# Feed-forward's first step: raw weights of the third and fourth pairs loaded ahead of the store of the last normalised rows

## The chip, the cores and the metric

The kernel runs on one core of one Trainium2 chip. The metric is the time of one execution in device microseconds (us). Three runs of the kernel before took 2641.86, 2644.74 and 2649.18 us; the median is 2644.74 us.

## The reference, cut to what matters

The program is a decoder trunk of two layers over 1024 tokens of width 1024, all in 32-bit floats. Each layer is a token mixer (latent attention in layer 0, a recurrent scan, RWKV-7, in layer 1) beside a memory attention, an output projection, a layer norm, a squared-ReLU feed-forward of width 4096, and a second layer norm:

```python
o = mixer(x @ w_in)                        # layer 0: attention; layer 1: RWKV scan
n = layer_norm(ALPHA * x + o @ w_out)      # these are the "normalised rows"
h = relu(n @ w_ff1) ** 2                   # first step of the feed-forward
x = layer_norm(ALPHA * n + h @ w_ff2)      # second step; reads n again
```

## The kernel before, in words

**Operands.** A 32-bit matrix is split into a high and a low part of a shorter type. ScalarE (ACT) casts the high part (L143), VectorE (DVE) subtracts it from the raw tile and writes the low part (L144). A product is then three TensorE (PE) matmuls for each tile of 128 rows: high by high, high by low, low by high. A row such as `N<-slot` of ACT L143 is the cast of the raw tile `slot` into a tile of the pool `N`; `N<-slot,N` of DVE L144 is the subtraction that belongs to it.

**The first step** is in `out_and_ff`, called once for each layer. The 1024 columns of w_ff1 by 1024 rows are multiplied with seven products of blocks instead of eight, after Strassen and Winograd, for each of 16 pairs `p` of column tiles. A pair needs products of raw blocks (A11 by B11, A12 by B21), and of sums of blocks: S3 by T3, S2 by T2, S1 by `TA`, S4 by B22, A22 by T4. The S are sums of weight blocks, formed on DVE in `blocks` (the four lines after the split of a22); the T are differences of the transposed normalised rows, formed in `second_half` and split into the tiles `TB` (T2 and T3). The rows are handled two tiles of 128 at a time, `tt` = 0, 2, 4, 6; T2 and T3 are whole only when `second_half(6, ...)` has been done.

**The early pairs.** For p = 0 to 3 the first two products (A11 by B11 and A12 by B21) run while the last rows are still being transposed: `early()` is a stream of matmuls from which `second_half` takes some between its transposes and the rest at its end. `ahead(p)` loads the raw A11 and A12 of one pair (512 KB) and splits them into `SR[0]`, two buffers that pairs 0 and 2, and 1 and 3, share. Pairs 0 and 1 land in the pool `wraw`, and their `ahead` is called before the stream. Pairs 2 and 3 land in the tile `slot` that later holds their result, and their `ahead`, the load included, is called inside the stream. In layer 0 the four slots of the pool hold the split output weights `wo[4]` and `wo[5]` until then.

**The normalised rows.** `norm` normalises two tiles of rows and stores them to the DRAM tensor `n_d`, which the second step reads again, hundreds of microseconds later. Its store is on SyncE's queue (SP), as are all loads of weights and the stores of the first step's results (`h_d`). SP takes its instructions in order: one that waits holds all behind it.

**What sets the order.** The program is not run in the order in which it is written. A scheduler with a cost model picks, for each engine, the order of the instructions over the whole program; `issue_after(x)` holds instructions back until `x` has been issued, `pin` keeps the order of matmuls as written. In layer 1 the output projection (`ps_o`, L149 to L151) is mixed by the scheduler with the matmuls of the scan, and the scan's matmuls in turn with the input projection (`ps_in`). The names `ps_y`, `ps_q` and `W` belong to the scan: `W` is its running state, updated on DVE from `ps_q` (L1202, L1209), and `ps_yo` (L1236) is a product on the scan's last result `yd` (L1222 to L1230) that ends in `o`, which is stored to `o_d` and loaded again as the last rows of the output projection's operand.

Of the kernel before, what the change touches and what calls it, by code (L numbers as in the profile page):

```python
# [10 lines left out]
F32 = mybir.dt.float32  # L11
# [9 lines left out]
P = 128  # L21
# [45 lines left out]
class Trunk:  # L67
# [74 lines left out]
    def split(self, hi, lo, src):  # L142
        h = self.nc.scalar.copy(hi, src)  # L143
        l = self.nc.vector.tensor_sub(lo, src, f32(hi))  # L144
        return h.ins, l.ins
# [1143 lines left out]
    def norm(self, R, tt, n_d):  # L1289
        r = R.t[tt // 4][:, tt % 4 : tt % 4 + 2, :]  # L1290
        chain = self.normalise2(r)
        self.nc.sync.dma_start(n_d[tt * P : (tt + 2) * P, :].rearrange("(t p) d -> p t d", p=P), r)
        return chain


    def out_part(self, ps, R, tt, nh, ws, first):
# [26 lines left out]
    def out_and_ff(self, layer, res_src, res_dst, last, R=None):  # L1323
        nc, a = self.nc, self.a
        n_d = self.dp.tile([T, D], F32, name=f"n_d{layer}") if R is None else self.n_d
# [5 lines left out]
        wv = a["w_ff1"][layer].rearrange("(k p) f -> p k f", p=P)  # L1331
        quad = lambda t: t.rearrange("p (a b) -> p a b", b=P)
        T0, T1 = slice(0, H), slice(H, T)
        with ExitStack() as s:
# [4 lines left out]
            slot = lambda dt=F32R: slp.tile([P, 1024], dt, name="slot", tag="slot")  # L1339

            def slot_pair():
                return slot(), slot()

            np_ = s1 = None
            with ExitStack() as s1:
# [9 lines left out]
                SR, we, cq, chain, EARLY = [], [], [], [], 4  # L1355
# [3 lines left out]
                def products(ps, A, B, fresh):  # L1359
                    for k in range(4):  # L1360
                        for i, (x, y) in enumerate(((0, 0), (0, 1), (1, 0))):
                            yield nc.tensor.matmul(ps, A[x][:, k, :], B[y][:, k, :], start=fresh and k == 0 and i == 0,  # L1362
                                                   stop=k == 3 and i == 2, skip_group_check=True)


                def ahead(p):
                    if not SR:
                        SR.append(region(0))
                    cq.append(slot(F32))
                    raw = cq[p] if p >= 2 else self.wr.tile([P, 1024], F32, name="wraw", tag="wraw")  # L1370
                    nc.sync.dma_start(quad(raw), wv[:, :, 2 * P * p : 2 * P * p + P])
                    z = SR[0][:, 2 * (p % 2), :], SR[0][:, 2 * (p % 2) + 1, :]
                    self.split(*z, raw)
                    we.append({"A11": [quad(t[:, 0:H]) for t in z], "A12": [quad(t[:, H:]) for t in z]})

                rawp = pool("traw1")
# [39 lines left out]
                with ExitStack() as s2:  # L1416
                    xq = pool_of(s2)("xq", side="right")
                    s3 = s2.enter_context(ExitStack())
                    rawp0 = pool_of(s3)("traw0")
                    s4 = s2.enter_context(ExitStack())  # L1420
                    pso = pool_of(s4)("pso", 2, space=PSUM)

                    B0 = [[p.tile([P, 4, 2 * P], F32, name=f"tr{q}{i}") for i in range(2)] for q, p in enumerate((rawp0, rawp))]
                    split = lambda Z, c, t: self.split(Z[0][:, :, c], Z[1][:, :, c], t)
                    span = lambda tt: (slice(tt * P, (tt + 2) * P), slice(tt % 4 * P, (tt % 4 + 2) * P), tt // 2 % 2)
                    rows_of = lambda tt: R.t[tt // 4][:, tt % 4 : tt % 4 + 2, :]

                    def norm(tt):  # L1430
                        chain.append(self.norm(R, tt, n_d))

                    def first_half(tt):
                        cs, es, i = span(tt)
                        for q, K in enumerate((K0, K1)):
                            self.columns(rows_of(tt), q, pst, B0[q][i], 2 * layer)
                            split(K, cs, B0[q][i])

                    def second_half(tt, between):
                        cs, es, i = span(tt)  # L1440
                        x0, x1, t = (xq.tile([P, 4, 2 * P], F32, name=n, tag=n, bufs=b) for n, b in (("x0", 2), ("x1", 1), ("xt", 1)))
                        for q, x in enumerate((x0, x1)):
                            self.columns(rows_of(tt), q, pst, x, 2 * layer, pin, between)

                        with self.tc.issue_after(chain[-1]):
                            nc.vector.tensor_sub(t, x1, x0)
                            split(T3, es, t)
                            nc.vector.tensor_sub(x0, x0, B0[0][i])
                            nc.vector.tensor_sub(t, x1, x0)
                            split(T2, es, t)  # L1450

                        def rest():
                            split(K1, cs, x1)
                            nc.vector.tensor_sub(B0[1][i], B0[1][i], t)

                        with self.tc.issue_after(chain[-1]):
                            if tt == 4:
                                rest()
                            split(K0, cs, x0)
                        return rest  # L1460

                    if R is None:
                        K1 = self.Xh.t[1], self.Xl.t[1]
                        R = Halves(new(0, F32), new(1, F32))
                        region = new
                        for tt in range(KT):
                            nc.sync.dma_start(R[:, tt, :], res_src[tt * P : (tt + 1) * P, :])
                        wo = []
                        for k in range(8):
                            to = (TB[k // 2][:, 2 * (k % 2), :], TB[k // 2][:, 2 * (k % 2) + 1, :]) if k < 4 else slot_pair() if k < 6 else self.split_pair()  # L1470
                            wo.append(self.load_into(a["w_out"][layer, k * P : (k + 1) * P, :], *to))
                        for h in (0, 4):
                            for tt in range(h, h + 4):
                                self.out_row(pso, R, tt, range(4), wo, True)
                            for tt in range(h, h + 4):
                                self.out_row(pso, R, tt, range(4, 8), wo[4:], False)
                                if tt % 2:
                                    norm(tt - 1)
                                    if tt < 4:
                                        first_half(tt - 1)  # L1480
                            if h == 0:
                                ahead(0)
                                ahead(1)
                    else:
                        K1 = new(0), new(1)
                        region = lambda i: self.x_tile("hl"[i], 1)
                        chain.append(self.chain)
                        for tt in (0, 2):
                            first_half(tt)
                        ahead(0)  # L1490
                        ahead(1)
                    s4.close()
                    psB = pool_of(s1)("psB", 4, space=PSUM)
                    cut = lambda t, c: (t[0][:, :, c], t[1][:, :, c])
                    B11, TA, B21, B22 = cut(K0, T0), cut(K0, T1), cut(K1, T0), cut(K1, T1)
                    As, todo = [], []


                    def early():
                        for p in range(EARLY):  # L1500
                            if p >= 2:
                                ahead(p)
                            c = cq[p][:, 0:H]
                            A, B = bank(psB, "ps_f"), bank(psA, "ps_f2")
                            yield from products(A, we[p]["A11"], B11, True)
                            nc.scalar.copy(c, A)
                            yield from products(B, we[p]["A12"], B21, True)
                            nc.vector.tensor_add(c, c, B)
                            As.append(A)
                            todo.append(p)  # L1510

                    stream = early()


                    def fill(*counts):
                        def between(g):
                            for _, m in zip(range(counts[g]), stream):
                                pin(m)
                        return between

                    second_half(4, fill(0, 6, 6, 16))
                    rest = second_half(6, fill(0, 6, 6, 99))
                    SR.append(region(1))
                    with self.tc.issue_after(chain[-1]):
                        w0 = blocks(0, self.wr)
                    rest()
                    s3.close()
                    wr2 = pool("wr2", 2)
                    self.wrs = [self.wr, wr2]
# [444 lines left out]
```

## Time and profile before

| | |
|---|---|
| median of three runs | 2644.74 us (2641.86 to 2649.18) |
| profiled execution | 2643.54 us, of which the span is 2641.8 us |
| mean granted clock of TensorE | 0.977 |
| busy: PE, DVE, ACT, POOL | 2515.6, 1788.9, 1194.4, 216.3 us |
| layer 0, start of the first step | about 570 to 625 us |
| layer 1, scan and start of the first step | about 1240 to 1960, and 1960 to 2060 us |

In the rows, the first number is the start in us from the span's start and the second is the time from the start to the end of the row's group; `x12` is the number of instructions in the group; what stands in square brackets is the engine's idle time just before, and the engine, tile and line that ended it. In the table of windows a line has the window, its length, and then the busy time of PE, of PE's weight loads, DVE, ACT and POOL with their numbers of instructions, the granted clock of TensorE, the share of DMA and GB/s.

### The profile page before, as it was taken

What the parts mean: (1) busy time and instruction counts of PE and PEld (TensorE: products, weight loads), DVE (VectorE), ACT (ScalarE), POOL (GpSimd) and SP (SyncE); (2) the same over time, 40 slices, a digit from 0 to 9 for tenths busy, and PEclk for the clock granted to TensorE, in tenths of its full rate; (3) what the DMA queues carried; (4) which work ended last, traced back from release to release, by engine and by line L of the source; (5) the groups of instructions that cost most, each with busy time, mean ns of one, the idle gap of its engine ahead of it and who ended that gap; (6) DMA issues with size and microseconds to landing.
All of it is one profiled execution on the core that took longest, in us unless ns stands there. A gap on an engine that the chain in (4) does not pass through costs nothing. (4 is left out here: it accounts for less than half of the span.)

```text
span 2641.8 us, 41840 instructions
## 1 busy us (share of the span) xinstructions
PE 2515.6 (95%) x16189; PEld 2040.3 (77%) x16189; DVE 1788.9 (68%) x3255; ACT 1194.4 (45%) x1964; POOL 216.3 (8%) x525
## 2 busy tenths in 40 slices
PE   8999999999999999999997999988977999999998
PEld 7877777777888888877876877776755888888886
DVE  5557766568665687676346777788558656678677
ACT  4465555254444433357543433455126444443343
POOL 0012233000000000000022112123000000000000
PEclk9999999999999999999998999999987999999999
DMA  4100001425443777545543333323313544486761
GB/s 171 59 27 11 15 18 47 144 92 175 147 150 139 268 288 265 198 152 183 205 140 75 107 91 100 97 74 100 132 71 109 172 147 151 148 339 240 260 239 64
DMA packets 276056, 370.54 MB, mean 140 GB/s; under 512 B 53841, under 2 KB 152785, under 8 KB 275857
## 3 DMA queue, kind: packets, MB, share of 16 engines
q1 hardware_dynamic: 275712, 367.61, 40.8%
q8 instruction: 127, 2.08, 0.3%
q14 instruction: 73, 0.59, 0.1%
q10 hardware_dynamic: 144, 0.26, 0.0%
HBM read 258.75 MB, written 109.05 MB: 139 GB/s over the span
## 5 line engine op out<-in xcount | busy, mean ns | idle before, releaser
L143 ACT CAST Xh<-wraw 128x1024 fp32r<-128x1024 f32 (+2 forms) x142 | 140.5, 1015 | 202.5 <-PE ps_z L1692 67.4
L149 PE MATMUL ps_in<-Xh,whi 128*128 128x512 f32 x480 | 195.0, 409 | 12.3 <-ACT whi L143 8.2
L150 PE MATMUL ps_in<-Xl,whi 128*128 128x512 f32 x480 | 192.1, 400 | 0.5 <-DVE Xl L144 0.5
L151 PE MATMUL ps_in<-Xh,wlo 128*128 128x512 f32 x480 | 192.3, 401 | 0.0
L143 ACT CAST Xl<-wraw 128x1024 fp32r<-128x1024 f32 x103 | 104.5, 1049 | 144.5 <-PE ps_z L1692 65.4
L144 DVE TENSOR_TENSOR Xh<-wraw,Xh 128x1024 fp32r<-128x1024 f32 x115 | 137.2, 1220 | 46.4 <-ACT Xh L143 41.7
L144 DVE TENSOR_TENSOR Xl<-wraw,Xl 128x1024 fp32r<-128x1024 f32 x103 | 123.4, 1220 | 44.0 <-ACT Xl L143 43.7
L144 DVE TENSOR_TENSOR wlo<-wraw,whi 128x1024 fp32r<-128x1024 f32 (+3 forms) x93 | 105.6, 1136 | 67.5 <-ACT whi L143 62.7
L143 ACT CAST whi<-wraw 128x1024 fp32r<-128x1024 f32 (+3 forms) x93 | 88.5, 953 | 117.3 <-PE ps_in L150 34.1
L149 PEld LDWEIGHTS ps_in<-Xh,whi 128*128 128x128 f32 x480 | 92.3, 192 | 34.2 <-ACT whi L143 8.2
L1362 PE MATMUL ps_f<-Xh,N 128*128 128x512 f32 x320 | 106.2, 396 | 4.9 <-ACT N L143 2.3
L151 PEld LDWEIGHTS ps_in<-Xh,wlo 128*128 128x128 f32 x480 | 91.9, 191 | 19.4 <-issue 0.2
L150 PEld LDWEIGHTS ps_in<-Xl,whi 128*128 128x128 f32 x480 | 91.9, 191 | 18.9 <-DVE Xl L144 1.0
L625 ACT ACTIVATE E<-ps_s,mx,SC 128x128 f32<-128x128 f32 (+7 forms) x96 | 79.4, 831 | 51.0 <-PE ps_pt L638 25.0
L628 POOL TENSOR_TENSOR E<-E,l 128x768 f32<-128x768 f32 (+5 forms) x60 | 82.9, 1384 | 203.0 <-DVE l L626 102.8
L1362 PE MATMUL ps_f<-TB,N 128*128 128x512 f32 x384 | 91.9, 389 | 1.0 <-ACT N L143 1.0
L1692 PE MATMUL ps_y<-Xh 128*128 128x512 f32 x384 | 90.1, 389 | 0.0
L1692 PE MATMUL ps_z<-Xl 128*128 128x512 f32 x384 | 89.6, 389 | 0.0
L1692 PE MATMUL ps_z<-Xh 128*128 128x512 f32 x384 | 89.6, 389 | 0.0
L1692 PE MATMUL ps_y<-Xh,Xh 128*128 128x512 f32 x360 | 85.0, 390 | 0.0
L1362 PEld LDWEIGHTS ps_f<-TB,N 128*128 128x128 f32 x384 | 72.0, 188 | 16.3 <-ACT N L143 1.4
L1692 PEld LDWEIGHTS ps_z<-Xl 128*128 128x128 f32 x384 | 72.1, 188 | 15.0
(520 smaller groups left out, 6546.7 us busy)
## 6 DMA issues: line engine op xcount, KB each, us to landing
wraw<-in_w_ff_dram SPq DMA_DIRECT2D x180, 512.0 KB
wraw<-h_d SPq DMA_DIRECT2D x108, 512.0 KB
h_d<-slot SPq DMA_DIRECT2D x128, 256.0 KB
h_d<-tr SPq DMA_DIRECT2D x64, 256.0 KB
wraw<-in_w_in_dram SPq DMA_DIRECT2D x31, 512.0 KB
lo_d<-l_st SPq DMA_DIRECT2D x36, 256.0 KB
rkv_d<-rkv_st SPq DMA_DIRECT2D x36, 256.0 KB
wraw<-in_w_out_dram SPq DMA_DIRECT2D x16, 512.0 KB
```

The source lines that it names most:

```text
L143: h = self.nc.scalar.copy(hi, src)
L144: l = self.nc.vector.tensor_sub(lo, src, f32(hi))
L149: mm(ps, wh, xh, start=first, stop=False)
L150: mm(ps, wh, xl, start=False, stop=False)
L151: mm(ps, wl, xh, start=False, stop=last)
L625: nc.scalar.activation(E3[:, g, :], S[:, g * w0 : g * w0 + n], AF.Exp, bias=mx[:, g : g + 1], scale=SC[:, i : i + 1], accum_out=l[:, g : g ...
L628: nc.gpsimd.tensor_mul(E3, E3, l[:, :, None].broadcast_to([P, nh, n]))
L1362: yield nc.tensor.matmul(ps, A[x][:, k, :], B[y][:, k, :], start=fresh and k == 0 and i == 0, stop=k == 3 and i == 2, skip_group_check=True)
L1692: m = nc.tensor.matmul(ps[t], A[x][:, u, t * P : (t + 1) * P], B[y][:, u, :], start=fresh and i == u == j == 0, stop=end and i == last_ an ...
```

## The change

The store of the normalised rows becomes a function of its own, `keep`; `norm` calls it for all rows but the last two tiles (tt = 6). The load of a pair's raw weights becomes a function `fetch`. After the `ahead` of pairs 0 and 1, in both layers, the raw weights of pairs 2 and 3 are fetched, and then the last rows are kept, held by `issue_after` until both loads have been issued. `ahead` of pairs 2 and 3, in the stream as before, only splits. No instruction is added or removed.

```diff
     def norm(self, R, tt, n_d):
         r = R.t[tt // 4][:, tt % 4 : tt % 4 + 2, :]
         chain = self.normalise2(r)
+        if tt < 6:
+            self.keep(R, tt, n_d)
+        return chain
+
+    def keep(self, R, tt, n_d):
+        r = R.t[tt // 4][:, tt % 4 : tt % 4 + 2, :]
         self.nc.sync.dma_start(n_d[tt * P : (tt + 2) * P, :].rearrange("(t p) d -> p t d", p=P), r)
-        return chain
...
+                def fetch(p):
+                    cq.append(slot(F32))
+                    raws.append(cq[p] if p >= 2 else self.wr.tile([P, 1024], F32, name="wraw", tag="wraw"))
+                    return nc.sync.dma_start(quad(raws[p]), wv[:, :, 2 * P * p : 2 * P * p + P])
 
                 def ahead(p):
+                    if p < 2:
+                        fetch(p)
...
-                    cq.append(slot(F32))
-                    raw = cq[p] if p >= 2 else self.wr.tile([P, 1024], F32, name="wraw", tag="wraw")
-                    nc.sync.dma_start(quad(raw), wv[:, :, 2 * P * p : 2 * P * p + P])
...
-                    self.split(*z, raw)
+                    self.split(*z, raws[p])
...
                         ahead(0)
                         ahead(1)
+
+                    with ExitStack() as st:
+                        for p in range(2, EARLY):
+                            st.enter_context(self.tc.issue_after(fetch(p).ins))
+                        self.keep(R, 6, n_d)
                     s4.close()
```

The scheduler then orders every engine anew. Three places follow in which the order of an engine differs.

First, SP's queue at the start of the first step of layer 0. L1371 before and L1376 now are the loads of raw weights, L1292 and L1299 the stores of normalised rows (`N_4711` holds tt = 4 and 6), L1385 and L1397 the loads of `blocks`, L1546 and L1563 stores of results. Before:

```order
L1371 DMA wraw<-in_w_ff_dram 128x8x128 x2
L1292 DMA n_d_4671<-N_4710 128x2x1024 x2
L1385 DMA wraw<-in_w_ff_dram 128x4x256 x2
L1292 DMA n_d_4671<-N_4711 128x2x1024 x2
L1546 DMA h_d_4672<-slot 128x512
L1371 DMA slot<-in_w_ff_dram 128x8x128 x2
```

Now:

```order
L1376 DMA wraw<-in_w_ff_dram 128x8x128 x2
L1299 DMA n_d_4671<-N_4710 128x2x1024 x2
L1397 DMA wraw<-in_w_ff_dram 128x4x256 x2
L1376 DMA slot<-in_w_ff_dram 128x8x128 x2
L1299 DMA n_d_4671<-N_4711 128x2x1024 x2
L1563 DMA h_d_4672<-slot 128x512
```

The two loads into slots have moved ahead of both stores of the rows tt = 4 and 6 and of one store of results. In layer 1 they have moved up too: from behind all four stores of normalised rows to behind the first of them.

Second, DVE in layer 0, at the two subtractions that finish T3 and T2 (the rows `TB_4690<-xt,TB_4689`). L1508 before is L1525 now (a pair's second product is added to its first), L1550 is L1567 (the squared ReLU of the sum), and L1404 is L1416 (a sum of weight blocks). Before:

```order
L144 TENSOR_TENSOR Xl_80<-x_5445,Xh_78 128x4x256
L1448 TENSOR_TENSOR x_5444<-x_5444,tr_4707 128x1024
L144 TENSOR_TENSOR TB_4690<-xt,TB_4689 128x4x256
L1508 TENSOR_TENSOR slot<-slot,ps_f_5502 128x512
L144 TENSOR_TENSOR Xl_79<-x_5444,Xh_77 128x4x256
L1449 TENSOR_TENSOR xt<-x_5445,x_5444 128x1024
L1550 SCALAR_TENSOR_TENSOR slot<-slot 128x512
L144 TENSOR_TENSOR wlo<-wraw,whi 128x512
L1454 TENSOR_TENSOR tr_4709<-tr_4709,xt 128x1024
L144 TENSOR_TENSOR TB_4690<-xt,TB_4689 128x4x256
```

Now:

```order
L1458 TENSOR_TENSOR xt<-x_5449,x_5448 128x1024
L1567 SCALAR_TENSOR_TENSOR slot<-slot 128x512
L1525 TENSOR_TENSOR slot<-slot,ps_f_5534 128x512
L1460 TENSOR_TENSOR x_5448<-x_5448,tr_4707 128x1024
L144 TENSOR_TENSOR TB_4690<-xt,TB_4689 128x4x256
L1567 SCALAR_TENSOR_TENSOR slot<-slot 128x512
L144 TENSOR_TENSOR Xl_79<-x_5448,Xh_77 128x4x256
L1461 TENSOR_TENSOR xt<-x_5449,x_5448 128x1024
L144 TENSOR_TENSOR wlo<-wraw,whi 128x512
L1466 TENSOR_TENSOR tr_4709<-tr_4709,xt 128x1024
L1416 TENSOR_TENSOR wraw<-wraw 128x4x128
L144 TENSOR_TENSOR TB_4690<-xt,TB_4689 128x4x256
```

Each of the two rows `TB` now stands behind three more operations on 512 columns than before, counted from the first row of the two tiles tt = 4 on: T3's behind L1525 twice and L1567 once, T2's behind L1525, L1567 and L1416. In the same part the two rows `N_5088<-slot` of pair 2 and pair 3 (`N_5091<-slot` now) have moved up by one place each, and ACT's casts that feed them by more: the first of them from behind six other operations to directly behind the two of L230 that normalise the last rows.

Third, PE at the end of layer 1's scan: the scan's last matmuls (`ps_y`), matmuls of the output projection (`ps_o`, one number for each of its accumulators) and the product on the scan's last result (`ps_yo`). Before, where the dots stand for the rest of 12 rows of `ps_o`:

```order
L151 MATMUL ps_o_18932<-whi_18262,Xl0_17441 128x512
L1167 MATMUL ps_y_18640<-W_17992,NR_17810 64x64 x4
L149 MATMUL ps_o_19010<-whi_18232,Xh0_17440 128x512
L150 MATMUL ps_o_19010<-wlo_18233,Xh0_17440 128x512
...
L151 MATMUL ps_o_19024<-whi_18242,Xl0_17441 128x512
L1236 MATMUL ps_yo_18784<-cst_75,yd_18639 64x64 x16
```

Now, where the dots stand for the rest of 36 such rows:

```order
L151 MATMUL ps_o_18918<-whi_18262,Xl0_17441 128x512
L1167 MATMUL ps_y_18640<-W_17992,NR_17810 64x64 x4
L149 MATMUL ps_o_18932<-whi_18232,Xh0_17440 128x512
L150 MATMUL ps_o_18932<-wlo_18233,Xh0_17440 128x512
...
L149 MATMUL ps_o_19010<-whi_18232,Xh0_17440 128x512
...
L151 MATMUL ps_o_19024<-whi_18242,Xl0_17441 128x512
L1236 MATMUL ps_yo_18784<-cst_75,yd_18639 64x64 x16
```

The number of matmuls is the same; 24 of `ps_o` that stood between the scan's last steps now stand behind its last matmul. Many rows of PE, DVE, ACT and POOL between 1240 and 1960 us have changed places in the same way, by a few matmuls or operations each.

More of the change, by code (lines that the diff above doesn't have):

```diff
@@ L1363, in products @@
                                                    stop=k == 3 and i == 2, skip_group_check=True)
+                raws = []
+                def fetch(p):
+                    cq.append(slot(F32))
+                    raws.append(cq[p] if p >= 2 else self.wr.tile([P, 1024], F32, name="wraw", tag="wraw"))
+                    return nc.sync.dma_start(quad(raws[p]), wv[:, :, 2 * P * p : 2 * P * p + P])
                 def ahead(p):
+                    if p < 2:
+                        fetch(p)
                     if not SR:
                         SR.append(region(0))
-                    cq.append(slot(F32))
-                    raw = cq[p] if p >= 2 else self.wr.tile([P, 1024], F32, name="wraw", tag="wraw")
-                    nc.sync.dma_start(quad(raw), wv[:, :, 2 * P * p : 2 * P * p + P])
                     z = SR[0][:, 2 * (p % 2), :], SR[0][:, 2 * (p % 2) + 1, :]
-                    self.split(*z, raw)
+                    self.split(*z, raws[p])
                     we.append({"A11": [quad(t[:, 0:H]) for t in z], "A12": [quad(t[:, H:]) for t in z]})
```

## The prediction

> **What bounds the kernel now.** I read the engines' busy times first, then the same by stretch, to see where TensorE (PE) does not run.
>
> ```profile
> PE 2515.6 (95%) x16189; PEld 2040.3 (77%) x16189; DVE 1788.9 (68%) x3255; ACT 1194.4 (45%) x1964; POOL 216.3 (8%) x525
> ```
>
> ```profile
> 570.00:625.00 55.00, 48.34 (x216) 38.33 (x216) 51.42 (x72) 37.70 (x53) 0.00 (x0) 0.97 0.47 153
> ...
> 1240.00:1500.00 260.00, 243.81 (x1927) 199.17 (x1927) 136.49 (x313) 118.58 (x219) 45.21 (x175) 0.96 0.42 130
> 1500.00:1850.00 350.00, 317.98 (x4244) 254.66 (x4244) 279.30 (x819) 164.25 (x384) 80.03 (x273) 0.97 0.34 94
> 1850.00:1960.00 110.00, 107.74 (x824) 81.62 (x823) 63.47 (x154) 16.41 (x23) 0.00 (x0) 1.00 0.27 96
> 1960.00:2060.00 100.00, 73.36 (x322) 56.32 (x321) 72.21 (x129) 56.87 (x83) 0.00 (x0) 0.80 0.36 119
> ```
>
> PE is busy 2515.6 us of a span of 2641.8, and its instructions do not change, so only its idle time (126 us) and its clock can. Of the idle time the five windows hold 6.7, 16.2, 32.0, 2.3 and 26.6 us (length less busy time). The window 570 to 625 is the first step of layer 0, and there DVE is busy 51.42 of 55 us, more than PE. For the sum I take each place where the change moves work that PE waits for.
>
> **Layer 0: what the early load is worth, and to whom.** The loads, the cast, and PE's waits, before:
>
> ```profile
> 571.62 9.51 SPq L1292 DMA_DIRECT2D n_d<-N  x2
> ...
> 584.00 1.20 SPq L1371 DMA_DIRECT2D slot<-in_w_ff_dram  x2
> ```
>
> ```profile
> 588.44 1.04 ACT L143 CAST N<-slot 128x1024 fp32r<-128x1024 f32 x1 [1.88 <-DMA slot<-in_w_ff_dram]
> ```
>
> ```profile
> 589.54 0.50 PE L1362 MATMUL ps_f<-Xh,N 128*128 128x512 f32 x1 [2.27 <-ACT N L143]
> ...
> 592.26 1.17 PE L1362 MATMUL ps_f<-Xh,N 128*128 128x512 f32 x2 [1.99 <-DVE N L144]
> ...
> 604.42 5.62 PE L1362 MATMUL ps_f<-TB,N 128*128 128x512 f32 x24
> 610.72 0.50 PE L1362 MATMUL ps_f<-Xh,N 128*128 128x512 f32 x1 [0.68 <-ACT cpair L1572]
> ...
> 614.72 1.20 PE L1362 MATMUL ps_f<-TB,N 128*128 128x512 f32 x4 [0.98 <-ACT N L143]
> ```
>
> SP stands 9.5 us at the stores of tt = 4 and 6, whose rows are not yet normalised, and only then loads pair 2 (584.00). ACT's cast waits for that load, and PE waits 2.27 us for the cast and 1.99 for the subtraction. With the loads ahead of both stores they leave at about 571.6 and take the 4.4 us that lie between 584.00 and 588.44, so they are there by 576 and the cast can run in its new place, behind the normalising that SP's stores waited for, about 581 (571.62 + 9.51). The 4.26 us of waits go, and so does a slow spell:
>
> ```profile
> 592.00:594.00 2.00, 1.74 (x4) 1.44 (x5) 2.00 (x4) 2.00 (x3) 0.00 (x0) 0.59 0.10 35
> 594.00:596.00 2.00, 2.00 (x6) 1.51 (x5) 2.00 (x2) 1.09 (x2) 0.00 (x0) 0.56 0.34 131
> ```
>
> The granted clock was 0.59 and 0.56 in these 4 us, which cost 2 × 0.41 + 2 × 0.44 = 1.7. The early stream thus ends about 6.0 us sooner, near 598.4 instead of 604.4.
>
> What PE needs next is T3, then T2, and those come from DVE:
>
> ```profile
> 577.09 0.69 DVE L144 TENSOR_TENSOR wlo<-wraw,whi 128x512 fp32r<-128x512 f32 x1
> 577.70 1.22 DVE L1446 TENSOR_TENSOR xt<-x,x 128x1024 f32<-128x1024 f32 x1
> 578.84 0.68 DVE L1404 TENSOR_TENSOR wraw<-wraw 128x512 f32<-128x512 f32 x1
> ...
> 599.54 1.22 DVE L144 TENSOR_TENSOR TB<-xt,TB 128x1024 fp32r<-128x1024 f32 x1
> ...
> 605.88 1.22 DVE L144 TENSOR_TENSOR TB<-xt,TB 128x1024 fp32r<-128x1024 f32 x1
> ...
> 615.31 1.22 DVE L144 TENSOR_TENSOR N<-wraw,N 128x1024 fp32r<-128x1024 f32 x1
> ```
>
> None of DVE's rows from 577.09 to 621 has an idle time in brackets: it runs without a gap, 0.61 us from one start to the next for 512 columns (577.09 to 577.70) and 1.14 for 1024. An earlier weight cannot make it faster; it only changes what comes first. Now three 512-column operations stand ahead of T3's last subtraction and three ahead of T2's that did not before (the order shown above): each is 1.8 us later. T3 is ready at 599.54 + 1.22 + 1.8 = 602.6, T2 at 605.88 + 1.22 + 1.8 = 608.9. PE, done at 598.4, idles 4.2 us, runs S3·T3 (12 matmuls of 5.62 / 24 = 0.234, so 2.8, more at the low clock that follows an idle spell), waits again to 608.9, and ends S2·T2 at 611.8. The copy adds 0.68 and S1·TA 2.8: 615.2, where before the next product began at 614.72. So the first step is 0.5 us later, 2.2 if S2·T2 falls into a slow spell like the one above. I take +1, nearer the former, because S3·T3 at the low clock would fill the wait ahead of T2 and keep PE busy; range 0 to +2.2. What ended last here was DVE, and it stays so.
>
> The Trainium skill (TensorE: Matmul & The Clock Gate, Part 1: The HAM clock gate) says that the clock halves after an idle window of about 3.4 us and is full again after about as long a busy time. The rows at 592 to 596 show a low clock of that length behind two waits of 2.27 and 1.99 with two matmuls between, so waits shorter than the page's window are enough when they follow closely; by its rule alone the first new gap would slow S3·T3 and the second not S2·T2, which gives the lower figure, +0.5.
>
> **Layer 1, same step.** Here the load was not late:
>
> ```profile
> 2002.56 1.83 SPq L1371 DMA_DIRECT2D slot<-in_w_ff_dram  x2
> ```
>
> ```profile
> 2013.92 1.07 ACT L143 CAST Xh<-slot 128x1024 fp32r<-128x1024 f32 x1
> ```
>
> ```profile
> 2019.98 1.22 PE L1362 MATMUL ps_f<-Xh,Xh 128*128 128x512 f32 x2 [2.94 <-DVE Xh L144]
> ...
> 2038.16 0.50 PE L1362 MATMUL ps_f<-TB,Xl 128*128 128x512 f32 x1 [1.76 <-ACT TB L143]
> 2041.76 4.94 PE L1362 MATMUL ps_f<-TB,Xl 128*128 128x512 f32 x11 [3.10 <-DVE TB L144]
> ```
>
> ```profile
> 2032.34 1.22 DVE L144 TENSOR_TENSOR TB<-xt,TB 128x1024 fp32r<-128x1024 f32 x1
> ...
> 2040.49 1.22 DVE L144 TENSOR_TENSOR TB<-xt,TB 128x1024 fp32r<-128x1024 f32 x1
> ...
> 2046.91 2.35 DVE L144 TENSOR_TENSOR Xh<-wraw,Xh 128x1024 fp32r<-128x1024 f32 x2
> ```
>
> The cast at 2013.92 waits for nothing; its place in ACT's order held it. In the new order it and its subtraction come sooner, so the 2.94 us go and the stream ends 3 us or so sooner, but T3, T2 and the first weights come from the same unbroken DVE: by its new order T3 is ready at 2033.2 (2033.6 before), T2 at 2040.7 (2041.7), the weights of row 2046.91 about 1.0 sooner. PE reaches the products on those weights at 2045 to 2047 and waits for them. I take −1; range −2.5 to +0.5. On SP the loads pass three stores of rows and a store of `o`; they would hold these up if their slots were not free, but the slots' last readers are `ps_y` matmuls of an earlier step of the scan, so I count nothing.
>
> **The end of the scan.** The change does not touch it; the scheduler's new order does, and this is the largest term.
>
> ```profile
> 1960.59 0.45 PE L1167 MATMUL ps_y<-W,NR 64*64 64x64 f32 x8
> ...
> 1963.64 0.39 PE L151 MATMUL ps_o<-whi,Xl 128*128 128x512 f32 x1
> 1969.20 1.97 PE L1236 MATMUL ps_yo<-cst,yd 64*64 64x64 f32 x32 [5.17 <-DVE yd L1230]
> 1978.65 0.79 PE L149 MATMUL ps_o<-whi,Xh 128*128 128x512 f32 x1 [7.48 <-ACT Xh L143]
> ```
>
> After the scan's last matmuls (done at 1961.04) come 12 of `ps_o`, the last of which starts at 1963.64, so 0.236 us from one to the next; then PE idles 5.17 us until `yd` has gone through DVE and ACT, and 7.48 us while the result goes to DRAM and back. With 24 of the `ps_o` moved behind the last scan matmul, that one comes 24 × 0.236 = 5.7 us sooner, at 1954.9. The chain from there to `ps_yo` takes the same 8.6 us (1960.59 to 1969.20) and ends at 1963.5, while PE has 36 × 0.236 = 8.5 us to fill it. `ps_yo` then starts near 1964.0, the 5.17 are gone, and the second wait starts as much sooner; ACT's normalising of the last rows may hold `o` for 0.4. I take −4.8; bounds −5.7 and +1, the latter if the scan's last steps, with fewer `ps_o` between them, wait themselves.
>
> **The start of the scan and its body.** The longest wait there:
>
> ```profile
> 1420.73 0.47 PE L1192 MATMUL ps_y<-W,ARK 128*64 128x64 f32 x2 [3.81 <-DVE W L1209]
> ```
>
> ```profile
> 1418.83 0.42 DVE L1088 SCALAR_TENSOR_TENSOR AR<-kk,pt 128x256 f32<-128x256 f32 x1 [4.43 <-POOL pt L1077]
> ...
> 1420.39 0.61 DVE L1209 TENSOR_TENSOR W<-ps_q,pC 64x128 f32<-64x128 f32 x2
> ```
>
> The update of `W` was ready but stood behind AR, which waited 4.43 us for POOL. In the new order it is ahead of AR. That removes at most the 3.81; but what AR feeds is not sooner, and some of the wait will return there. I take −2, half; bounds −3.8 and 0. The rest of the 48 us of idle time between 1240 and 1850 is several dozen waits of 0.2 to 3.7 us whose places are newly drawn. By the view of waits the largest sets are
>
> ```profile
> PE ps_q L1206 <- DVE W L1202: 10.5, 12, 1.9
> PE ps_q L1143 <- DVE XT L1139: 6.6, 3, 3.7
> PE ps_y L1192 <- DVE W L1209: 6.4, 5, 3.8
> ```
>
> (total, number, longest). I see no sign in them that one order is better and take 0, with ±5 as an estimate: half of the first set gone, or half as much again.
>
> **The sum.** +1 − 1 − 4.8 − 2 = −6.8 against the profiled execution of 2643.54: 2636.7. That execution is 1.2 below the median 2644.74, against which runs will be compared, so 2637.9; I say 2638.
>
> **Rivals.** (a) *Nobody takes the gain back.* If the order in which DVE works were no limit, the early stream's 6.0 us in layer 0 and the same kind of gain in layer 1 (2.94 plus half of a slow spell, some 5) would stay: with the scan's −6.8, 2644.7 − 17.8 = 2627. Against it stands DVE without a gap up to T2. (b) *The scan's new order is worth nothing*: filler behind the last step only moves waits into the steps ahead. With the feed-forward's +1 − 1 the time is 2645. For it: the window before 1960 has only 2.3 us of PE idle, so the last steps had little cover to spare. (c) *Slower*: one mechanism, the state `W`. Each scan step waits for DVE's copy (L1202) unless other matmuls lie between; 12 such waits cost 10.5 us. If fillers moved to the end uncover eight more steps at the longest of them, 1.9 us each, +15, less the tail's 4.8 and with nothing at the start of the scan: 2655. It decides from seven more such waits on (13 − 4.8 is about 8). Against it: 15 or more `ps_o` stand in every gap of the last steps in the new order, at 3.5 us. (d) *The change does not do what it says*: in layer 1 the load was not waited for; this is in the −1 already.
>
> **Chances and range.** A measurement here tells about 0.3%, 7.9 us, so faster means below 2636.8 and slower above 2652.6. The forecast (2633 to 2642) 0.47; (a) 0.12, (b) 0.32, (c) 0.09. Of the forecast's 0.47 somewhat over half lies above 2636.8, so faster is 0.21 + 0.12 and some of the ±5 of (b), 0.36 in all; slower is 0.09, same 0.55. For 8 in 10 the range leaves out half of (a) below and most of (c) above: 2627 to 2650.
>
> **What would show it.** Right: the loads into `slot` at 571 to 573 us, the cast `N<-slot` without a wait for a DMA near 581, no PE wait at 589 and 592; then a new PE wait of about 4 us on `TB` L144 near 598 and another of 1 to 4 near 606; DVE still without a gap; in layer 1 the wait at 2020 gone and a longer one ahead of T3; `ps_yo` at the end of the scan with next to no wait. Wrong: T3's subtraction before 600 (rival a); 5 us of waits on `W` or `yd` that stand elsewhere in the last 100 us of the scan (rival b); a dozen more waits on L1202 (rival c).

## The result: slower by 0.86%, lost in layer 1's scan

The changed kernel took 2665.84 us (median of 6 runs, 2664.37 to 2669.71) beside 2645.09 us of the kernel before (6 runs on the same chip): a ratio of 1.0086, 95% interval 1.0076 to 1.0097. That is 22.7 us slower (20.1 to 25.7); the two medians differ by 20.8, the spans of the two profiled executions by 22.8. In the groups of runs further down, single runs at a far longer time (3138.71 us in e5, 3543.57 in e6, 4930.89 in e7, 3679.5 of before beside them) are not in the ratios. The prediction said 2638 us and 2627 to 2650.

The busy times after, and two of the stretches that the prediction shows for before:

```profile
PE 2521.8 (95%) x16189; PEld 2041.3 (77%) x16189; DVE 1790.3 (67%) x3255; ACT 1194.7 (45%) x1964; POOL 219.5 (8%) x525
```

```profile
570.00:625.00 55.00, 48.12 (x213) 37.09 (x212) 50.31 (x70) 38.15 (x53) 0.00 (x0) 0.97 0.45 149
...
1500.00:1850.00 350.00, 303.90 (x3867) 244.06 (x3863) 261.76 (x758) 149.22 (x343) 81.41 (x269) 0.92 0.33 91
```

The span is 2664.6, 22.8 longer: PE is idle 142.8 us instead of 126.2 (+16.6) and busy 6.2 more for the same 16189 matmuls, at a mean granted clock of 0.975 instead of 0.977. The window 1500 to 1850 shows both: PE busy 303.90 instead of 317.98, the clock 0.92 instead of 0.97, and 377 fewer matmuls done (3867 for 4244). The stretch 570 to 625, which the diff edits in layer 0, is nearly as it was; the time went elsewhere.

**The first step of layer 0** came out as the prediction drew it. SP, ACT, PE and DVE after:

```profile
569.90 0.99 SPq L1376 DMA_DIRECT2D slot<-in_w_ff_dram  x2
572.18 9.52 SPq L1299 DMA_DIRECT2D n_d<-N  x2
```

```profile
581.21 1.04 ACT L143 CAST N<-slot 128x1024 fp32r<-128x1024 f32 x1
```

```profile
600.79 0.50 PE L1368 MATMUL ps_f<-TB,N 128*128 128x512 f32 x1 [1.43 <-ACT TB L143]
603.18 4.75 PE L1368 MATMUL ps_f<-TB,N 128*128 128x512 f32 x12 [1.89 <-DVE TB L144]
609.53 2.79 PE L1368 MATMUL ps_f<-TB,N 128*128 128x512 f32 x11 [1.60 <-DVE TB L144]
...
615.86 1.07 PE L1368 MATMUL ps_f<-TB,N 128*128 128x512 f32 x4
```

```profile
601.90 1.23 DVE L144 TENSOR_TENSOR TB<-xt,TB 128x1024 fp32r<-128x1024 f32 x1
...
608.25 1.22 DVE L144 TENSOR_TENSOR TB<-xt,TB 128x1024 fp32r<-128x1024 f32 x1
```

The loads leave ahead of both stores and the cast waits for no transfer. PE's waits at 589 and 592 are gone, and new ones stand ahead of T3 and T2, which DVE delivers at 603.13 and 609.47 (predicted: 602.6 and 608.9). The row of four that began at 614.72 begins at 615.86; the trace was already 0.6 late just ahead of the step (DVE's row of 577.70 stands at 578.27), so the step cost 0.5.

**The body of the scan** is where it went. The view of DVE's waits from 1240 to 1990, first of before, then of after (total, number, longest):

```profile
DVE XT L1139 <- DMA X<-xd: 11.0, 5, 4.9
...
DVE rkv_st L703 <- DMA rkv_d<-rkv_st: 1.9, 2, 1.6
```

```profile
DVE XT L1139 <- DMA X<-xd: 33.4, 7, 7.0
DVE rkv_st L703 <- DMA rkv_d<-rkv_st: 16.7, 5, 6.9
```

Two kinds of transfer that were mostly hidden are now waited for. The first is an exchange through DRAM that each chunk of the scan makes: SP stores `nd` (L1114), loads it as `nb`, POOL solves a triangular system of 14 steps on it (L1117 to L1123, `substitute`), SP stores the result as `xd` (L1125) and loads it as `X` (L1128), and DVE transposes it to `XT` (L1139). The rows of one such exchange, SP and DVE, before:

```profile
1528.18 1.22 SPq L1114 DMA_DIRECT2D nd<-NR  x2
...
1548.61 1.53 SPq L1128 DMA_DIRECT2D X<-xd  x2
...
1556.79 0.43 DVE L1139 STREAM_TRANSPOSE XT<-X 128x256 f32<-128x256 f32 x1
```

and the same exchange after:

```profile
1549.53 1.43 SPq L1114 DMA_DIRECT2D nd<-NR  x2
...
1570.40 2.85 SPq L1125 DMA_DIRECT2D xd<-xb  x8
1573.42 0.49 SPq L1128 DMA_DIRECT2D X<-xd  x1
...
1578.02 0.45 DVE L1139 STREAM_TRANSPOSE XT<-X 128x256 f32<-128x256 f32 x1 [6.65 <-DMA X<-xd]
```

From the store of `nd` to `XT` pass 28.5 us now and 28.6 before. Before, DVE filled them with 20.1 us of its own work and 7.5 us of waits for PE and ACT, and when it came to `XT`, 8.2 us after the load of `X` had left SP, the data was there. Now it has 18.3 us of work and 2.5 us of such waits, comes to `XT` 28.49 − 6.65 = 21.8 us after the store, and stands for the rest. In this exchange the trip itself is longer too: the load of `X` leaves 23.9 us after the store instead of 20.4. Over all twelve exchanges it is not: 22.3 us on average before and 22.4 now. What is shorter is the time until DVE comes to `XT` (the time to `XT` less the wait): 28.9 us on average before, 25.8 now, and 21.3 to 22.8 in the five exchanges that wait longest. The other four of these wait 4.89, 7.04, 5.42 and 5.04 us.

The second is one store. SP's queue around 1500, after and then before:

```profile
1496.70 0.35 SPq L716 DMA_DIRECT2D rkv_d<-rkv_st  x1
1510.69 2.85 SPq L1125 DMA_DIRECT2D xd<-xb  x8
...
1515.96 5.88 SPq L716 DMA_DIRECT2D rkv_d<-rkv_st  x2
```

```profile
1496.61 2.85 SPq L1125 DMA_DIRECT2D xd<-xb  x8
...
1501.27 0.59 SPq L716 DMA_DIRECT2D rkv_d<-rkv_st  x1
```

SP stands 13.6 us at the store of `xd`, which POOL has not finished, and the store of `rkv_st` stands behind it. DVE needs that buffer again, and `W`'s update and PE stand behind DVE (this is 6.9 of the 16.7 us; the others are four waits of 1.2 to 3.5 us at 1272 to 1350, which e7 below still has, with 9.1 us):

```profile
1520.72 0.75 DVE L703 SCALAR_TENSOR_TENSOR rkv_st<-pr,omu,pm 128x512 f32<-128x512 f32 x1 [6.91 <-DMA rkv_d<-rkv_st]
...
1522.14 0.60 DVE L1209 TENSOR_TENSOR W<-ps_q,pC 64x128 f32<-64x128 f32 x2
```

```profile
1522.47 0.47 PE L1192 MATMUL ps_y<-W,ARK 128*64 128x64 f32 x2 [6.54 <-DVE W L1209]
```

That these two are the cause, and that the scan's new order made them, is what the experiments had to show.

### The profile page after: what moved, and what is told of

Read it like the earlier page. It is cut to its first block, busy times and chain, and to the rows that moved or that the text cites. A ratio compares the mean times of both kernels' runs of the same rounds, so it can differ in the third digit from the quotient of the medians.

```text
span 2664.6 us, 41852 instructions
## 1 busy us (share of the span) xinstructions
PE 2521.8 (95%) x16189; PEld 2041.3 (77%) x16189; DVE 1790.3 (67%) x3255; ACT 1194.7 (45%) x1964; POOL 219.5 (8%) x525
## 5 line engine op out<-in xcount | busy, mean ns | idle before, releaser
L149 PE MATMUL ps_in<-Xh,whi 128*128 128x512 f32 x480 | 196.3, 411 | 12.5 <-ACT whi L143 8.7
L151 PEld LDWEIGHTS ps_in<-Xh,wlo 128*128 128x128 f32 x480 | 92.8, 193 | 20.1 <-issue 0.5
```

Of the source, the lines that this page charges most:

```text
L149: mm(ps, wh, xh, start=first, stop=False)
L151: mm(ps, wl, xh, start=False, stop=last)
```

## The experiments

The times of all runs, as ratios to runs of before on the same chip: 2645.09 us beside the changed kernel, 2642.58 beside e1 to e4, 2641.29 beside e5 to e8, 2643.64 beside e9 and e10. The names of the theories in the quoted expectations are those of that time; "the exchange" is what A1 stands for in them.

| run | what it is | us | ratio, 95% interval |
|---|---|---|---|
| after | the change | 2665.84 | 1.0086 (1.0076 to 1.0097) |
| e1_old_scan_order | the change, scan ordered as before | 2641.17 | 0.9995 (0.9984 to 1.0006) |
| e2_new_scan_order | before, scan ordered as after | 2665.34 | 1.0088 (1.0065 to 1.0110) |
| e3_layer0_only | the change in layer 0 alone | 2666.08 | 1.0083 (1.0055 to 1.0112) |
| e4_layer1_only | the change in layer 1 alone | 2641.46 | 0.9996 (0.9984 to 1.0008) |
| e5_half_new | after, half of POOL's steps | 2637.10 | 0.9979 (0.9966 to 0.9992) |
| e6_half_old | before, half of POOL's steps | 2633.15 | 0.9966 (0.9953 to 0.9979) |
| e7_one_store | after, one store moved on SP | 2651.85 | 1.0041 (1.0027 to 1.0054) |
| e8_act_relu | e1, a DVE operation moved to ACT | 2637.53 | 0.9986 (0.9977 to 0.9996) |
| e9_tail | e1, 24 matmuls moved to the scan's end | 2646.12 | 1.0009 (1.0000 to 1.0018) |
| e10_tail_relu | e9 with e8's edit | 2639.93 | 0.9986 (0.9978 to 0.9995) |

### The edit without the new order, and the new order without the edit

The order of the scan (the second half of layer 1's mixer, all engines) is written down as a table for each engine and imposed by dependencies that need no semaphore. e1 is the change with before's order of the scan, e2 the kernel before with the changed kernel's order (the diff in part):

```diff
+    for engine, text in tables.items():
+        own = [...]                                # the engine's instructions in the scan
+        order = _order(text)                       # places in the program's text
+        for x, y in zip(order, order[1:]):
+            tc.add_manual_dep(own[y], own[x].name, ..., reason="order")   # ... stands for the class NoSync
```

> The change in both layers, with every engine's order inside layer 1's scan (the instructions written in rwkv) queued as in the kernel before. Theory A, the scan's new order costs the time: 2644 to 2648 us, that is +1 to +2 from layer 0 and -1 from layer 1 against before; the wait of 5.2 us on yd at the scan's end is back. Theory B, the moved loads and the late store cost it themselves, wherever their traffic lands: stays at 2660 to 2666.

> The kernel before, no load or store moved, with every engine's order inside the scan queued as in the changed kernel. Theory A: 2662 to 2668 us, with the waits of DVE on X (5 to 7 us each, five times) and on the staging buffer (6.9 us) where the changed kernel has them. Theory B: 2643 to 2648.

e1 stands at 0.9995 and e2 at 1.0088. The order alone costs the whole 22 to 23 us, and the edit with the old order costs nothing that can be measured. In e2's trace the same waits are there:

```profile
DVE XT L1139 <- DMA X<-xd: 29.6, 7, 6.2
DVE rkv_st L703 <- DMA rkv_d<-rkv_st: 14.7, 7, 7.4
```

### Which half of the edit redraws the order

The change made in one layer alone (the diff in part; in the other layer, `norm` stores the last rows as before, and `keep` and the early `fetch` are not called):

```diff
-                    if p < 2:
+                    if p < 2 or layer != 0:        # e3; e4: layer != 1
                         fetch(p)
```

> The change in layer 0 alone; the scheduler gives the scan the same order as in the changed kernel, and layer 1's first step its old one. Theory A: 2664 to 2669 us, as the changed kernel or 1 us above. Theory B, if the loss comes from layer 1's loads passing the stores at the scan's end: 2643 to 2648; if it comes from layer 0's: as A.

> The change in layer 1 alone; the scan keeps the order of the kernel before. Theory A: 2642 to 2646 us, before less about 1 us. Theory B with the loss in layer 1's loads: 2660 to 2666; with the loss in layer 0's: as A.

Layer 0 alone gives 1.0083, and its scan comes out in the changed kernel's order; layer 1 alone gives 0.9996, with the scan in the old one. So the edit that is 700 us ahead of the scan, and that cost 0.5 us where it stands, is the one that costs 22. Why the scheduler's choice there tips with it was not looked into.

### POOL's steps halved, under either order

If it is the exchange's round trip that DVE waits for, a shorter trip must give back much under the new order and little under the old one. Both kernels leave out every second step of the substitution (their results are those of an incomplete solve); the order of every engine is held otherwise:

```diff
-                    for t in range(1, 15):
+                    for t in range(1, 15, 2):
```

> The changed kernel with every engine's scan order kept as it is, but every second step of POOL's substitution left out (its result is then another; 7 of 14 steps, about 5 us of POOL for each of 12 exchanges). Theory A1, the new order leaves too little work between the store of NR and the first use of X, so that DVE stands 5 to 7 us in each of five exchanges and PE behind it: 15 to 22 us faster than the changed kernel, 2644 to 2651. Theory A2, the new order is worse by many small waits that have nothing to do with the exchange: 3 to 6 us faster, 2660 to 2663.

> The kernel before with the same steps of the substitution left out and every engine's scan order kept. A1: the old order covers the exchange, so little is left to gain: 3 to 6 us faster than before (one wait of 4.9 us and four of 1.3 to 1.7). A2: as much as the changed kernel gains, 3 to 6 us. Told apart by the difference of the two runs, some 12 to 16 us less between them under A1 and none under A2.

Under the new order it gave back 1.0086 − 0.9979 = 1.07%, 28 us; under the old one 0.34%, 9 us. Both are more than was expected, but the difference of 19 us (14 to 25 by the intervals) is most of the 22.7. The 19 us are not the exchange alone: with POOL done sooner, the store of `rkv_st` that stands behind `xd` leaves sooner as well. And both gains hold something that the expectations did not have: the wait of AR for POOL at the scan's start (5.65 us after, 4.43 before) is 0.8 in e5 and gone in e6. The waits left in e5, and in e6:

```profile
DVE XT L1139 <- DMA X<-xd: 14.2, 5, 3.9
DVE rkv_st L703 <- DMA rkv_d<-rkv_st: 9.8, 4, 3.4
```

```profile
DVE XT L1139 <- DMA X<-xd: 3.9, 1, 3.9
DVE rkv_st L703 <- DMA rkv_d<-rkv_st: 0.2, 1, 0.2
```

e5's remaining 3 to 4 us over e6 stand with its remaining waits. That the old order gains 9 us too says that the exchange was not wholly hidden before either.

### One store

In e7 one instruction of SP's queue moves, and nothing else on any engine:

```diff
 # SP's queue at 1497 to 1516 us of the changed kernel
+ rkv_d<-rkv_st
  xd<-xb x8
  X<-xd x2
  wraw<-in_w_in_dram
- rkv_d<-rkv_st
```

> The changed kernel with one instruction moved on one queue: on SP, the first store of rkv_st after the xd stores at 1510.69 goes ahead of them, all else as in the changed kernel. If SP's standing for POOL there holds the staging buffer, DVE's wait of 6.9 us at 1520.72 and PE's 6.5 at 1522.47 go: 4 to 6.5 us faster than the changed kernel. If something else sets that place: within 1 us of it.

The ratio fell from 1.0086 to 1.0041: 12 us for one store (7 to 16 by the two intervals), where 4 to 6.5 were expected. Its trace has the store ahead of `xd`, and the exchange quoted above ends 11.8 us sooner (1578.02 to 1566.23), while DVE's wait at it stays:

```profile
1492.54 13.00 SPq L716 DMA_DIRECT2D rkv_d<-rkv_st  x2
1506.54 2.85 SPq L1125 DMA_DIRECT2D xd<-xb  x8
```

```profile
1566.23 0.45 DVE L1139 STREAM_TRANSPOSE XT<-X 128x256 f32<-128x256 f32 x1 [6.84 <-DMA X<-xd]
```

Of the 11.8 us, 4.1 were there ahead of the moved store: an `XT` that starts at 1475.21 us in the changed kernel starts at 1471.07 in e7, though the two have the same order up to there. At its own place the store is thus worth 7.7 us: the wait of 6.9, and the rest goes with the half clock behind it (last section), where e7 has full clock. What the ratios show above that was traced to no row. Single traces of one order differ by as much: between DVE's rows at 1232 and at 1910 us, e2 takes 7.9 us less than the changed kernel, with the same order of the scan.

The view of DVE's waits has 33.2 us on `X<-xd` in e7 and 33.4 in the changed kernel. So the two causes are apart: the store is 8 to 12 of the 22.7 us, and the remaining 11 to 15 go with the exchanges. This second share is a remainder; no run takes away the exchanges' waits alone.

### DVE in layer 0's first step

The prediction held that DVE sets T3 and T2, so that an early load alone cannot help. In e8, which is e1 otherwise, the squared ReLU of the early pairs runs on ACT:

```diff
                 for p in todo:
-                    relu2(cq[p][:, 0:H])
+                    relu2_act(cq[p][:, 0:H])
```

> The change with the old scan order (as e1) and the squared ReLU of the four early pairs on ACT instead of DVE, some 2 us less of DVE ahead of T3 and T2. If DVE is what takes the gain back in layer 0: T3 and T2 ready 1.8 to 2.4 us sooner, and the products on them as much; 1 to 3 us faster than e1 in all, seen in the trace more than in the time. If ACT, with two operations for each, becomes the bound: T3 and T2 not sooner, and no gain.

```profile
600.79 2.79 PE L1368 MATMUL ps_f<-TB,N 128*128 128x512 f32 x11 [0.77 <-DVE TB L144]
...
607.99 6.05 PE L1368 MATMUL ps_f<-TB,N 128*128 128x512 f32 x15 [2.15 <-DVE TB L144]
```

The same in e1, of which e8 is the edit:

```profile
603.36 4.45 PE L1368 MATMUL ps_f<-TB,N 128*128 128x512 f32 x12 [1.90 <-DVE TB L144]
609.71 4.36 PE L1368 MATMUL ps_f<-TB,N 128*128 128x512 f32 x11 [1.90 <-DVE TB L144]
```

T3's product starts at 600.79 instead of 603.36 and without the low clock (2.79 for eleven, not 4.45 for twelve); T2's starts at 607.99 instead of 609.71, but at the low clock in both (6.05 for fifteen, 4.36 for eleven, 0.40 each). The next row on `TB` starts 1.0 us sooner (616.62 for 617.64). So DVE set the start of both products. The time is 0.9986 of before's, 0.0009 below e1's, some 2 us; the interval of e8 (0.9977 to 0.9996) excludes 1, that of the difference to e1 was not measured. This version is faster than both kernels.

### The end of the scan alone

> The change with the old order of the scan on PE, SP and POOL, except that 24 ps_o matmuls stand behind the scan's last ps_y instead of ahead of it; DVE and ACT are left to the scheduler. It isolates the term 'end of the scan' (-4.8) of the prediction. The theory that this term was right: the wait of 5.2 us ahead of ps_yo goes, the wait for the transposed rows behind it stays at 7.5 to 9, and the time is 3 to 5 us below that of the old scan order alone (2641.2), so 2636 to 2638. The rival, prediction's case (b): the 24 matmuls are missed in the last steps, 5 us of waits on W or yd stand there, and the time is 2641 again. Where DVE's free order has made an exchange late, waits on X<-xd of more than 2 us would show in the body and the time would be above 2641.

> The kernel with the shortened scan end, and with the early pairs' squared ReLU taken from DVE to ACT. If the two gains lie at different places and add up (3 to 5 us from the scan's end, 3.6 us measured for the ReLU on ACT), the time is 2632 to 2635, the fastest of all kernels here that compute everything. If either is not additive, it stays at 2637 to 2638.

The edit is to e1's table for PE: 24 `ps_o` from the scan's last steps go behind its last `ps_y`; DVE and ACT are left to the scheduler, so the end is not changed alone. e9 came out at 1.0009, above e1's 0.9995 by little more than the noise, and e10 at e8's 0.9986, so the shorter end brought no gain that shows. (The 3.6 us that e10's expectation calls measured is a difference of medians from two chips; by the ratios it is some 2.) Its rows in e9:

```profile
1971.99 1.15 PE L1236 MATMUL ps_yo<-cst,yd 64*64 64x64 f32 x32 [1.42 <-DVE ln_t L226]
1983.71 0.80 PE L149 MATMUL ps_o<-whi,Xh 128*128 128x512 f32 x1 [10.58 <-ACT Xh L143]
```

The 5.2 us ahead of `ps_yo` shrink to 1.42, but the next wait grows from 7.4 to 10.58: 12.5 us become 12.0, because ACT normalises two pairs of rows (2.4 us each) ahead of `o`. Against e1, e9 is 6.5 us late ahead of this end (an `XT` at 1896.27 and at 1902.79) and 5.0 behind it (1978.69 and 1983.71). The largest loss that was found lies elsewhere, where DVE's order, left to the scheduler, has the copy of `W` ahead of an earlier `yd` (L1230). PE's row for `ps_yo` there and the window around it, first in e1 and then in e9:

```profile
1564.69 1.15 PE L1236 MATMUL ps_yo<-cst,yd 64*64 64x64 f32 x32 [1.51 <-DVE yd L1230]
```

```profile
1564.00:1568.00 4.00, 3.31 (x52) 2.65 (x53) 2.52 (x8) 1.02 (x2) 0.00 (x0) 1.00 0.00 0
```

```profile
1565.52 1.97 PE L1236 MATMUL ps_yo<-cst,yd 64*64 64x64 f32 x32 [2.50 <-DVE yd L1230]
```

```profile
1564.00:1568.00 4.00, 2.48 (x33) 2.28 (x34) 1.39 (x5) 0.46 (x1) 0.00 (x0) 0.65 0.00 0
```

One operation of 0.6 us placed first makes the wait 1.0 longer, the clock falls from 1.00 to 0.65, and the next `XT` is 3.0 us later (1568.60 in e1, 1571.57 in e9), having been 0.2 sooner before. The two profiled executions are 10.5 us apart (spans 2638.5 and 2649.0), where the ratios put 3.7 us (0.0014) between e1 and e9; e9's is the slowest of its runs. So this place has 3 of the 10.5, and the rest was not taken apart. e9's longest wait on an exchange (7.29 us) comes later, at an `XT` that starts at 1657.41 instead of 1653.45, in a chunk that is by then some 3.4 us late; it adds half a microsecond.

## Why the prediction was wrong

**Layer 0, +1 (0 to +2.2): right.** +0.5, by its own steps: DVE's unbroken row, T3 and T2 later, a low clock in S3·T3. In e1 the same S2·T2 fell into the low clock (4.36 us for 11 matmuls, for 2.79 above), the other end of that range: there the step cost 2.2.

**Layer 1, −1: right in this trace.** −1.3 (the lag went from 24.1 to 22.8); in e1, with the same edit, DVE's rows gain 3.3 from the scan's end to the kernel's, more than the range had. The wait of 2.94 is gone and a longer one stands ahead of T3:

```profile
2057.01 5.36 PE L1368 MATMUL ps_f<-TB,Xl 128*128 128x512 f32 x12 [4.16 <-DVE TB L144]
```

**The scan's end, −4.8: nearly, inside the changed kernel.** `ps_yo` has no wait, the next wait is longer, since ACT's normalising holds `o` until 1995.39, 1.3 us after `ps_yo` is done, and not the 0.4 allowed for:

```profile
1993.12 2.37 ACT L230 ACTIVATE Xl<-Xl,ln_t,ln_y 128x1024 f32<-128x1024 f32 x2 [2.37 <-DVE ln_t L228]
1995.39 1.00 ACT L1239 ACTIVATE o<-ps_yo,vec 128x256 f32<-128x256 f32 x2
```

```profile
1992.96 1.15 PE L1236 MATMUL ps_yo<-cst,yd 64*64 64x64 f32 x32
2002.82 0.80 PE L149 MATMUL ps_o<-whi,Xh 128*128 128x512 f32 x1 [8.71 <-ACT Xh L143]
```

12.65 us of waits became 8.71, so −3.9. As a gain by itself it is not shown: e9 did not find it.

**The scan's start, −2: wrong, +0.9.** The update of `W` still stands behind AR, AR waits longer for POOL, and PE's wait behind it is 4.75 us instead of 3.81:

```profile
1426.36 0.43 DVE L1088 SCALAR_TENSOR_TENSOR AR<-kk,pt 128x256 f32<-128x256 f32 x1 [5.65 <-POOL pt L1077]
...
1427.15 0.61 DVE L1209 TENSOR_TENSOR W<-ps_q,pC 64x128 f32<-64x128 f32 x2
```

**The rest of the scan, "I see no sign in them that one order is better and take 0, with ±5": this is the step that failed.** It measured about +25, against the 5 of its bound: the row behind the tail is 24.2 late (1978.65 to 2002.82), less the 2.4 by which the trace is late where the scan begins (1232.23 to 1234.64 on DVE) and the 0.9 of the start, plus the 3.9 that the tail gave, 24.8. The ±5 was taken from PE's waits on `W` (L1202) alone, as was rival (c), and those did not move: 10.5 us before, 10.2 after. What moved were DVE's waits, which the prediction does not quote: 11.0 us before and 33.4 after on `X<-xd`, 1.9 and 16.7 on the store of `rkv_st`. PE's waits show them in part. The set on `XT` L1139 that the prediction quoted with 6.6 us is 5.2 after, with 5.4 more on `ml` L795, the row that DVE has behind an `XT` that came late; the set on `W` L1209 went from 6.4 to 14.0.

The risk could have been seen beforehand. Before, five exchanges already waited for 11.0 us in all, and in nine of the twelve `XT` starts 3.6 to 5.7 us after the load of `X` leaves, about as soon as where it waits for it (3.6 to 5.4); so the trip was about as long as the time beside it and had next to no slack. The store could not be read from before's waits (1.9 us in all); what puts it behind `xd` is the new order of SP's queue in the scan, of which the prediction quotes nothing.

**The rivals.** (a) 2627 fell as argued: T3 did not come before 600, and e8 shows that DVE was the limit. (b) 2645 is what the edit is worth with the old order (e1, 0.9995), though not for (b)'s reason. (c) had the sign and the wrong mechanism. The chance of 0.09 for slower rested on one rival out of the scan's many.

## What to carry to other kernels

Where a scheduler draws the order of the whole program, an edit is worth its own effect plus that of the new order everywhere, and the second can be the larger: compare the orders over the whole program and on every queue, or hold the order of what the edit should not touch. Of each round trip through DRAM in a loop, ask how much other work stands between its first store and its last use; where this equals the trip, an order that takes work out of the gap can cost time. A store that waits for a slow engine delays all stores behind it on its queue, and one of them may be what frees a buffer.

## What the runs showed of the hardware

One wait of 6.54 us on PE (to 1522.47) is followed by some 4 us at half clock and then by full clock:

```profile
1522.00:1524.00 2.00, 1.53 (x22) 1.43 (x23) 1.94 (x7) 0.00 (x0) 0.00 (x0) 0.50 0.34 131
1524.00:1526.00 2.00, 2.00 (x17) 1.58 (x15) 1.90 (x9) 0.00 (x0) 0.00 (x0) 0.50 0.40 133
1526.00:1528.00 2.00, 2.00 (x10) 1.65 (x9) 0.40 (x3) 0.00 (x0) 0.00 (x0) 0.95 0.45 148
```

The Trainium skill (TensorE: Matmul & The Clock Gate, Part 1: The HAM clock gate) has such a halving after about 3.4 us of idleness and a recovery after about as long a busy time; this trace agrees. In layer 0, though, two waits of 1.43 and 1.89 us with half a microsecond of work between them were enough (the twelve matmuls behind took 4.75 us), and in e9 one of 2.50 was (0.65 over the 4 us around it), at the place where e1's 1.51 was not (1.00). Near the edge it is not settled by the program: the eleven matmuls of S2·T2 took 2.79 us in the changed kernel and 4.36 in e1, which have the same program there, after waits of 1.60 and 1.90. So in e9 a wait of one microsecond more went with three of delay, and the 7.7 us of one store are more than its wait of 6.9.
